# Scaling the FFN input in one VectorE step, and a block's sums of squares at another place, in a hybrid decoder layer

## The chip, the cores and the metric

One core of one Trainium2 chip. The metric is the device time of one execution in microseconds (us); the kernel before ran three times, and one further execution was profiled.

## What is computed

The whole layer works on 2048 tokens of 1024 channels in float32. The part that matters here is the second half and its border with the first:

```python
x = x + jnp.concatenate([hm, hp], axis=-1) @ w_out      # output projection of the mixer
h = rmsnorm(x, g_ffn)                                   # x * rsqrt(mean(x*x) + EPS) * g
up = causal_dwconv(h @ w_up, w_ffn_conv) + b_ffn_conv   # 1024 -> 5632, conv over 3 tokens
gate, val = up[..., :D_FF], up[..., D_FF:]
x = x + (jax.nn.silu(gate) * val) @ w_down              # 2816 -> 1024
return rmsnorm(x, final_norm)
```

## The kernel before, in words

Channels lie on the 128 partitions, tokens along a tile. A tile is 128x512: one of KT = 8 groups of channels (`k`) for one of NB = 4 blocks of 512 tokens (`b`). A float32 product is made of three float32r matmuls (`products`, L112 to L114), since each operand is split in a rounded part (a cast on ScalarE, `split_h`, L94) and a rest (a subtraction on VectorE, `split_l`, L100). So every operand of TensorE costs one ScalarE and one VectorE step first; the split tiles are called `whl` (weights of the first half), `w` (weights of the FFN) and `s` (activations of the FFN).

**Order of the work.** Everything is issued by hand in one program order. TensorE's loops call `tick()` every few matmuls; each tick runs one step of every side stream, a Python generator (`sides`). `yield from wait(n)` puts a stream n ticks back, `until(flag)` holds it, `need(flag)` ticks until a flag is set. What the ticks issue stands in the engines' in-order queues in that order, and semaphores do the rest.

**Mixer and its end.** For each block `in_phase` projects the input; `out_proj(b)` then multiplies with `w_out` in two halves of four channel groups, each in its own PSUM bank `big` (there are four). `evacuate` (L948) adds the residual, loaded as `xr` (three buffers), and a DMA of ScalarE writes the sum to the DRAM scratch `x2d`. `squares` then squares the tile into the same `big` bank (L919) and adds it to `ss` (L923, L925): the bank is free for the next product only after that addition. With all eight tiles added, `scale2` turns `ss` into the scale 1/sqrt(mean) (`spread_rsqrt`: a matmul with ones, then Ln, Exp and Square on ScalarE) and writes it to `r2d`. For the last block `ss` goes to scratch `s2d`, and `last_scale` makes the scale 100 ticks later, in the middle of the first up part.

**FFN.** Tokens are taken in two halves of 1024, in the order `up_half(0)`, `down(0)`, `down(1)`, `up_half(1)`, `down(2)`, `down(3)`. An up part is a Strassen-like scheme with seven products (A11, S1, S2, A12, S3, A22, S4) for each of 22 groups of output channels. Product A11 goes to a bank that `after` copies (ScalarE, L1359) before S2 adds to the same bank, so S2 waits for that copy. The operands of the seven products are 28 tiles. `b_first` makes them for the first half, during `out_proj(3)`, in whose first half `at` starts it: it loads the scale `rr` and 16 tiles of `x2d`, multiplies each with its channel weight and with `rr` (`b_scale`: a ScalarE step, L1138, and a GpSimd step, L1139), subtracts (`sub`, L1142, four of them on GpSimd) and splits. `b_prep(1)` does the same for the second half, during `down(1)`. `a_prep` loads and splits the operands of the down parts, `w_stream` those of the weights, up to nine ahead.

**End.** `squares2` squares and adds each finished output tile, each step after the one before it; `final` scales a block and writes it out. For the last block `down_last` computes the last channel group in two pieces of 256 tokens, and `final_part` scales all eight groups of a piece: five in one VectorE step each, three (1, 3, 5) with a ScalarE copy made earlier and a GpSimd step.

The change touches `out_proj`, `b_scale`, `sub`, `b_first`, `b_prep`, `last_scale`, `down`, `down_last`, `final_part` and `squares2`.

## Time and profile before

| | |
|---|---|
| Median of three runs | 2073.81 us (2069.91 to 2076.69) |
| The profiled execution | 2070.96 us |
| Its span, first to last instruction | 2069.2 us |
| PE matmul busy | 1986.1 us, 96%, x8948 |
| DVE (VectorE) busy | 1457.3 us, 70%, x2330 |
| ACT (ScalarE) busy | 1047.1 us, 51%, x1844 |
| POOL (GpSimd) busy | 236.5 us, 11%, x266 |
| Mean granted clock | 0.984 |

One execution was recorded. Times in rows are us from the span's start; engines are PE, DVE, ACT, POOL, and SP, whose queue issues most DMAs. "L948" is line 948 of the kernel. Matmuls overlap: a 128x512 one is listed with 0.39 us, and in full flow the next begins 0.23 us later. Busy shares are means over stages with different limits. The releaser behind an idle time is the instruction whose end allowed the next to start.

### The profile page before, as it was taken

The numbers are of one execution on the slowest core, as the hardware profiler recorded it, in microseconds if no ns is written. First come the engines' busy times: TensorE is split into PE (matmuls) and PEld (weight loads), VectorE is DVE, ScalarE is ACT, GpSimd is POOL, SyncE is SP. The second block draws the span as 40 slices with busy tenths as digits, with TensorE's granted clock in tenths as the row PEclk, the third lists the DMA queues.
The fourth block names the chain that finished last, engine by engine and source line by source line (L and its number), as shares of the span: only waits on it lengthen the run. The fifth ranks groups of instructions, "written<-read, shape, count | busy, mean of one in ns | idle before, by whom it ended". The sixth has DMA issues, their size and how long they took to land.

```text
span 2069.2 us, 24627 instructions
## 1 busy us (share of the span) xinstructions
PE 1986.1 (96%) x8948; PEld 1628.5 (79%) x8948; DVE 1457.3 (70%) x2330; ACT 1047.1 (51%) x1844; POOL 236.5 (11%) x266
## 2 busy tenths in 40 slices
PE   8999999998998699999999999989999999999997
PEld 6777877776886588788888888877888888888886
DVE  6587777777686977777878656577787787765433
ACT  5656655655644554544455444354455445544331
POOL 1004002012021500000000001120111111000001
PEclk9999999999999799999999999999999999999999
DMA  5433443452346313122224745432322222474441
GB/s 189 151 107 116 153 153 121 133 170 67 113 133 227 113 57 107 66 92 92 69 84 147 253 160 183 143 103 104 104 67 92 92 71 83 133 271 159 150 120 54
DMA packets 116954, 258.64 MB, mean 125 GB/s; under 512 B 9568, under 2 KB 27488, under 8 KB 116832
## 3 DMA queue, kind: packets, MB, share of 16 engines
q1 hardware_dynamic: 111504, 247.37, 36.2%
q10 hardware_dynamic: 5328, 9.70, 1.2%
q8 instruction: 70, 1.15, 0.2%
q14 instruction: 52, 0.43, 0.1%
HBM read 215.81 MB, written 41.22 MB: 124 GB/s over the span
## 4 chain that ended last, share of the span: by engine, by line
PE 77%; DVE 11%; ACT 5%; DMA 4%; issue 2%; SPq 1%; DVEq 0%; POOL 0%; ACTq 0%; POOLq 0%
PE big L112 21%; PE big L113 21%; PE big L114 21%; PE num L114 4%; PE num L113 4%; PE num L112 4%; DVE whl L100 1%; DVE s L100 1%; ACT hjunk L819 1%; DMA x<-x2d 1%; DVE tmp L519 1%; PE mm L503 1%; DVE w L100 1%; DVE hT L102 1%; ACT whl L94 1%
## 5 line engine op out<-in xcount | busy, mean ns | idle before, releaser
L112 PE MATMUL big<-s,w 128*128 128x512 f32 (+1 forms) x1562 | 609.3, 390 | 29.7 <-ACT r L1359 17.6
L114 PE MATMUL big<-s,w 128*128 128x512 f32 (+1 forms) x1562 | 606.7, 388 | 0.0
L113 PE MATMUL big<-s,w 128*128 128x512 f32 (+1 forms) x1562 | 606.5, 388 | 0.0
L94 ACT CAST w<-raw 128x512 fp32r<-128x512 f32 (+1 forms) x442 | 272.7, 619 | 502.8 <-PE big L114 378.1
L100 DVE TENSOR_TENSOR w<-raw,w 128x512 fp32r<-128x512 f32 (+1 forms) x442 | 306.2, 695 | 219.6 <-ACT w L94 214.5
L112 PEld LDWEIGHTS big<-s,w 128*128 128x128 f32 x1562 | 295.6, 189 | 94.3 <-ACT r L1359 19.6
L114 PEld LDWEIGHTS big<-s,w 128*128 128x128 f32 x1562 | 295.4, 189 | 60.5
L113 PEld LDWEIGHTS big<-s,w 128*128 128x128 f32 x1562 | 295.7, 189 | 59.4 <-issue 0.7
L1331 DVE SCALAR_TENSOR_TENSOR q<-q,vec 128x1024 f32<-128x1024 f32 x176 | 225.4, 1281 | 22.2 <-ACT q L1328 20.7
L112 PE MATMUL num<-s,w 128*128 128x512 f32 x396 | 154.7, 391 | 0.0
L114 PE MATMUL num<-s,w 128*128 128x512 f32 x396 | 154.2, 389 | 0.0
L113 PE MATMUL num<-s,w 128*128 128x512 f32 x396 | 154.1, 389 | 0.0
L112 PE MATMUL big<-hT,whl 128*128 128x512 f32 x320 | 130.3, 407 | 15.0 <-DVE ss L925 6.9
L100 DVE TENSOR_TENSOR whl<-wraw,whl 128x1024 fp32r<-128x1024 f32 x92 | 117.3, 1275 | 31.3 <-ACT whl L94 30.2
L100 DVE TENSOR_TENSOR s<-x,s 128x512 fp32r<-128x512 f32 x120 | 83.4, 704 | 70.6 <-ACT s L94 70.1
L113 PE MATMUL big<-hT,whl 128*128 128x512 f32 x320 | 127.9, 400 | 0.6 <-DVE hT L102 0.6
L114 PE MATMUL big<-hT,whl 128*128 128x512 f32 x320 | 127.7, 399 | 0.5 <-DVE whl L100 0.5
L94 ACT CAST s<-x 128x512 fp32r<-128x512 f32 x120 | 72.9, 619 | 106.1 <-PE big L114 48.0
L1328 ACT ACTIVATE q<-q,vec 128x1024 f32<-128x1024 f32 x88 | 109.4, 1243 | 0.0
L1352 POOL COPY q<-halo 128x2 f32<-128x2 f32 x88 | 64.4, 749 | 362.5 <-DVE q L1331 295.8
L112 PE MATMUL big<-whl,hT 128*128 128x512 f32 x256 | 105.0, 410 | 0.0
L113 PE MATMUL big<-whl,hT 128*128 128x512 f32 x256 | 101.9, 398 | 1.4 <-DVE whl L100 1.4
(268 smaller groups left out, 3002.4 us busy)
## 6 DMA issues: line engine op xcount, KB each, us to landing
raw<-in_w_up SPq DMA_DIRECT2D x44, 1024.0 KB, 5.7
raw<-in_w_down SPq DMA_DIRECT2D x35, 1024.0 KB, 5.1
wraw<-in_w_in SPq DMA_DIRECT2D x60, 512.0 KB, 3.3
act<-q SPq DMA_DIRECT2D x44, 512.0 KB, 6.5
x<-act SPq DMA_DIRECT2D x88, 256.0 KB, 3.9
wraw<-in_w_out SPq DMA_DIRECT2D x32, 512.0 KB, 3.3
xr<-in_xT SPq DMA_DIRECT2D x32, 256.0 KB, 4.1
x2d<-xr ACTq DMA_DIRECT2D x32, 256.0 KB, 2.9
```

The source lines that it names most:

```text
L94: act.copy(out=h, in_=src)
L100: dve.tensor_tensor(out=l, in0=src, in1=f(h), op=ALU.subtract)
L102: dve.scalar_tensor_tensor(out=l, in0=src, scalar=scale, in1=f(h), op0=ALU.mult, op1=ALU.subtract)
L112: pe.matmul(o, lhsT=lh, rhs=rh, start=first and i == 0, stop=False, skip_group_check=on)
L113: pe.matmul(o, lhsT=lh, rhs=rl, start=False, stop=False, skip_group_check=on)
L114: pe.matmul(o, lhsT=ll, rhs=rh, start=False, stop=last and i == n - 1, skip_group_check=on)
L503: pe.matmul(gp, lhsT=wg[:, k], rhs=hT[k][:, i], start=k == 0 and i == 0, stop=k == KT - 1 and i == 1)
L519: dve.scalar_tensor_tensor(out=y, in0=pre[:, n:n + BT], scalar=tap[n], in1=y, op0=ALU.mult, op1=ALU.add)
L819: act.activation(junk, nums[h // 2][:, h % 2, 0:DV], AF.Square, scale=rd[:, h:h + 1], accum_out=ssq[:, h:h + 1])
L1328: act.activation(y[gv], pre[gv][:, 2:2 + HT], AF.Identity, scale=tap[2], bias=vec[:, V_FB + ch:V_FB + ch + 1])
L1331: dve.scalar_tensor_tensor(out=y[gv], in0=pre[gv][:, n:n + HT], scalar=tap[n], in1=y[gv], op0=ALU.mult, op1=ALU.add)
L1352: pool.tensor_copy(t[:, 0:2], halo[:, gv * NJ + j])
```

## The change

In order of the program:

- The last block's squares leave `out_proj(3)`; `s2d`, its store, its load and `last_scale` go. Instead `late_scale(3)`, started with `down(0)`, loads the eight tiles of `x2d` again, one every five ticks into two buffers, squares (ScalarE) and adds (VectorE) them, makes the scale and sets the flag `r2`, for which `b_prep(1)` now waits.
- `b_scale` is one VectorE step (`scalar_tensor_tensor`: tile times channel weight times scale) in place of a ScalarE and a GpSimd one, 32 times in all. The four subtractions on GpSimd go to VectorE.
- `b_first` issues its loads six ticks after its start instead of at once, and scales, subtracts and splits in one stream.
- `squares2` no longer waits for the step before it, but four ticks, and adds a tick later.
- The last scaling takes eight VectorE steps; the three ScalarE copies and GpSimd steps go.

```diff
                 if k == KT - 1:
-                    flags.add(("ss", b))
-                    if b < NB - 1:
-                        sides.add(scale2(b, state["ss"], "prs"))
-                    else:
-                        act.dma_start(s2d, state["ss"])
+                    sides.add(scale2(b, state["ss"], "prs"))
...
                     act.dma_start(x2d[k // 2][b][:, k % 2], xr[k])
-                    sides.add(squares(k, o))
+                    if b < NB - 1:
+                        sides.add(squares(k, o))
...
         def b_scale(x, k, r):
-            act.activation(x, x, AF.Copy, scale=vec[:, V_FFN + k:V_FFN + k + 1])
-            pool.tensor_tensor(out=x, in0=x, in1=r, op=ALU.mult)
...
+            dve.scalar_tensor_tensor(out=x, in0=x, scalar=vec[:, V_FFN + k:V_FFN + k + 1], in1=r, op0=ALU.mult, op1=ALU.mult)
...
         def b_first():
-            rr = [ff1.tile([P, 2, 512], F32, tag=f"w{NW1 - 1}", name="rr")]
+            yield from wait(6)
+            rr = ff1.tile([P, 2, 512], F32, tag=f"w{NW1 - 1}", name="rr")
...
             load(0)
             load(1)
-            yield from wait(2)
-            sides.add(scaled())
-            yield from wait(5)
+            yield from wait(3)
...
                 if p < 4:
-                    yield from until("x2", p, kk)
+                    if kk == 0 and p < 2:
+                        load(2 + p)
+                    kh, a = XS[p]
+                    b_scale(x[p, kk], kk + 4 * kh, rr[:, a])
...
                 elif p == S2:
-                    sub(x[1, kk], x[2, kk], x[1, kk], pool)
+                    sub(x[1, kk], x[2, kk], x[1, kk])
...
         def b_prep(hh):
+            yield from until("r2", NB - 1)
...
         out_proj(NB - 1, at)
-        need("ss", NB - 1)
...
-        def last_scale():
-            r = ff2.tile([P, BT], F32, tag="ss", name="r")
-            sp.dma_start(r, s2d)
-            yield from wait(100)
-            yield from spread_rsqrt(r, f(ones_r), [r])
-            act.dma_start(r2d[NB - 1], r)
-        sides.add(last_scale())
+        def late_scale(b):
+            def load(k):
+                t = ff2.tile([P, 512], F32, tag=f"r{1 + k % 2}", name="t")
+                sp.dma_start(t, x2d[k // 2][b][:, k % 2])
+                return t
+            s, t = ff2.tile([P, 512], F32, tag="r0", name="s"), load(0)
+            for k in range(KT):
+                after = load(k + 1) if k + 1 < KT else None
+                yield from wait(3)
+                act.activation(t if k else s, t, AF.Square)
+                yield
+                if k:
+                    dve.tensor_tensor(out=s, in0=t, in1=s, op=ALU.add)
+                t = after
+                yield
+            yield from spread_rsqrt(s, f(ones_r), [s], (6, 2, 1, 1))
+            act.dma_start(r2d[b], s)
+            flags.add(("r2", b))
...
             sides.add(acc_load())
+            if b == 0:
+                sides.add(late_scale(NB - 1))
...
-            for k in (1, 3, 5):
-                x = acc[k // 2][:, k % 2]
-                need("sq", b, k)
-                act.activation(x, x, AF.Copy, scale=vec[:, V_FIN + k:V_FIN + k + 1])
...
-                if k in (1, 3, 5):
-                    pool.tensor_tensor(out=x, in0=x, in1=r, op=ALU.mult)
-                else:
-                    dve.scalar_tensor_tensor(out=x, in0=x, scalar=vec[:, V_FIN + k:V_FIN + k + 1], in1=r, op0=ALU.mult, op1=ALU.mult)
+                dve.scalar_tensor_tensor(out=x, in0=x, scalar=vec[:, V_FIN + k:V_FIN + k + 1], in1=r, op0=ALU.mult, op1=ALU.mult)
...
-                yield from until("sq", b, k - 1)
-                ss = state["ss"]
+                yield from until("sq", b, 0)
+                yield from wait(4)
                 slot = yield from take("mm")
                 o = bank([P, BT])
                 act.activation(o, x, AF.Square)
                 yield
-                dve.tensor_tensor(out=ss, in0=o, in1=ss, op=ALU.add)
+                yield
+                dve.tensor_tensor(out=state["ss"], in0=o, in1=state["ss"], op=ALU.add)
```

How the order of instructions moves, at three places. The lines after the change are numbered a few lower.

**SP's queue at the start of `b_first`**, in the first half of `out_proj(3)`: before.

```order
L1034 DMA raw<-in_w_up 128x2x1024
L937 DMA xr<-in_xT 128x512 x2
L1150 DMA rr<-r2d_89 128x512
L1150 DMA rr<-r2d_90 128x512
L1160 DMA xh<-x2d_0_73 128x512 x2
L1160 DMA xh<-x2d_0_77 128x512 x2
L1160 DMA xh<-x2d_1_74 128x512 x2
L1160 DMA xh<-x2d_1_78 128x512 x2
L226 DMA wraw<-in_w_out 128x1024
L937 DMA xr<-in_xT 128x512 x2
```

Now:

```order
L1030 DMA raw<-in_w_up 128x2x1024
L932 DMA xr<-in_xT 128x512 x2
L225 DMA wraw<-in_w_out 128x1024
L932 DMA xr<-in_xT 128x512 x2
L225 DMA wraw<-in_w_out 128x1024
L932 DMA xr<-in_xT 128x512
L1146 DMA rr<-r2d_89 128x512
L1146 DMA rr<-r2d_90 128x512
L1156 DMA xh<-x2d_0_73 128x512 x2
```

The next weights (`wraw`) and three more residual tiles (`xr`) stand ahead of the ten loads of scale and tiles, no longer behind them.

**DVE, first operands of the FFN** (`s`), in the second half of `out_proj(3)`: before.

```order
L100 TENSOR_TENSOR s<-xh,s 128x512
L100 TENSOR_TENSOR whl<-wraw,whl 128x1024
L100 TENSOR_TENSOR s<-xh,s 128x512
L925 TENSOR_TENSOR ss<-big,ss 128x512
L100 TENSOR_TENSOR s<-xh,s 128x512
L1142 TENSOR_TENSOR xh<-xh 128x512
L100 TENSOR_TENSOR s<-xh,s 128x512
L100 TENSOR_TENSOR whl<-wraw,whl 128x1024
L1142 TENSOR_TENSOR xh<-xh 128x512
L100 TENSOR_TENSOR s<-xh,s 128x512
L1142 TENSOR_TENSOR xh<-xh 128x512
L100 TENSOR_TENSOR s<-xh,s 128x512
```

Now (L1134 is the new scaling, L1137 the subtraction):

```order
L1134 SCALAR_TENSOR_TENSOR xh<-xh,vec,rr 128x512 x2
L100 TENSOR_TENSOR s<-xh,s 128x512
L1134 SCALAR_TENSOR_TENSOR xh<-xh,vec,rr 128x512
L100 TENSOR_TENSOR s<-xh,s 128x512
L100 TENSOR_TENSOR whl<-wraw,whl 128x1024
L1134 SCALAR_TENSOR_TENSOR xh<-xh,vec,rr 128x512
L100 TENSOR_TENSOR s<-xh,s 128x512
L1134 SCALAR_TENSOR_TENSOR xh<-xh,vec,rr 128x512
L1137 TENSOR_TENSOR xh<-xh 128x512
L100 TENSOR_TENSOR s<-xh,s 128x512
L1134 SCALAR_TENSOR_TENSOR xh<-xh,vec,rr 128x512
L1137 TENSOR_TENSOR xh<-xh 128x512
```

The additions to `ss` are gone, and a scaling step stands ahead of each subtraction.

**ACT at the border of `down(1)` and `up_half(1)`**: before (L1553 are the squares of `squares2`, L1359 the copy of A11, which stands behind the fourth of them).

```order
L94 CAST w<-sum 128x512
L1553 ACTIVATE mm<-q 128x512
L94 CAST s<-x 128x512
L94 CAST w<-raw 128x512
L1553 ACTIVATE mm<-q 128x512 x2
L94 CAST w<-raw 128x512
L1553 ACTIVATE mm<-q 128x512
L1359 COPY r<-big 128x512
```

Now:

```order
L94 CAST w<-sum 128x512
L94 CAST s<-x 128x512
L94 CAST w<-raw 128x512 x2
L1359 COPY r<-big 128x512
L1550 ACTIVATE mm<-q 128x512 x2
L94 CAST w<-raw 128x512
L1550 ACTIVATE mm<-q 128x512 x2
```

The copy now stands ahead of the four squares, behind one more cast of weights.

## Rows read from the trace of the kernel before

**Rows 1.** Busy time by stretch: us, then per engine busy us (instructions), granted clock, DMA share, GB/s

```profile
650.00:700.00 50.00, 35.79 (x145) 28.23 (x144) 39.50 (x40) 24.61 (x40) 27.38 (x18) 0.89 0.63 221
...
700.00:750.00 50.00, 40.29 (x155) 32.56 (x156) 42.05 (x62) 26.93 (x46) 5.48 (x10) 0.83 0.21 74
...
800.00:900.00 100.00, 95.88 (x409) 78.32 (x409) 75.47 (x96) 52.27 (x75) 3.40 (x16) 0.97 0.23 76
...
900.00:1000.00 100.00, 100.00 (x442) 82.64 (x441) 76.71 (x98) 49.90 (x73) 5.55 (x24) 1.00 0.29 94
...
1300.00:1400.00 100.00, 92.93 (x403) 76.54 (x402) 63.83 (x89) 45.28 (x77) 20.82 (x16) 0.97 0.33 113
...
705.00:722.00 17.00, 12.29 (x35) 9.46 (x36) 16.97 (x29) 10.69 (x20) 0.00 (x0) 0.70 0.37 127
...
1120.00:1140.00 20.00, 20.00 (x90) 16.57 (x89) 18.19 (x26) 15.65 (x26) 0.87 (x4) 1.00 0.69 236
```

**Rows 2.** Timeline, PE, 662 to 1396: start, us, operation, [idle before <- releaser]

```profile
670.90 0.79 PE L112 MATMUL big<-hT,whl 128*128 128x512 f32 x1 [6.93 <-DVE ss L925]
...
705.34 0.80 PE L112 MATMUL big<-s,w 128*128 128x512 f32 x1 [12.15 <-DVE ss L925]
...
717.49 0.80 PE L112 MATMUL big<-s,w 128*128 128x512 f32 x1 [4.37 <-ACT r L1359]
...
864.51 0.79 PE L112 MATMUL big<-s,w 128*128 128x512 f32 x1 [4.12 <-ACT r L1359]
...
1395.34 0.80 PE L112 MATMUL big<-s,w 128*128 128x512 f32 x1 [7.07 <-ACT r L1359]
```

**Rows 3.** Timeline, SP's DMA queue, 648 to 664

```profile
651.36 10.20 SPq L1160 DMA_DIRECT2D xh<-x2d  x8
...
662.10 0.91 SPq L937 DMA_DIRECT2D xr<-in_xT  x2
```

**Rows 4.** Timeline, DVE, 650 to 720

```profile
650.54 1.23 DVE L100 TENSOR_TENSOR whl<-wraw,whl 128x1024 fp32r<-128x1024 f32 x1 [0.19 <-ACT whl L94]
...
658.94 0.68 DVE L948 TENSOR_TENSOR xr<-big,xr 128x512 f32<-128x512 f32 x1
...
672.50 0.80 DVE L100 TENSOR_TENSOR s<-xh,s 128x512 fp32r<-128x512 f32 x1 [0.45 <-ACT s L94]
...
709.41 0.67 DVE L100 TENSOR_TENSOR s<-xh,s 128x512 fp32r<-128x512 f32 x1
```

**Rows 5.** Groups by form, DVE, 661.4 to 704.1: xcount | busy us, mean ns

```profile
L100 DVE TENSOR_TENSOR s<-xh,s 128x512 fp32r<-128x512 f32 x12 | 15.8, 1316 | 0.5 <-ACT s L94 0.5
...
L1142 DVE TENSOR_TENSOR xh<-x,xh 128x512 f32<-128x512 f32 x4 | 6.4, 1604 | 0.0
```

**Rows 6.** DMA issues, 640 to 720: xcount, KB each, median us to landing

```profile
x2d<-xr ACTq DMA_DIRECT2D x8, 256.0 KB, 2.7
...
xh<-x2d SPq DMA_DIRECT2D x12, 256.0 KB, 4.5
```

**Rows 7.** Timeline, DVE, 1412 to 1419: the operation that the new scaling uses

```profile
1415.84 1.41 DVE L1572 SCALAR_TENSOR_TENSOR q<-q,vec,rn 128x512 f32<-128x512 f32 x2
```

**Rows 8.** Timeline, ACT, 714 to 718

```profile
716.85 0.58 ACT L1359 COPY r<-big 128x512 f32<-128x512 f32 x1
```

**Rows 9.** Timeline, ACT, 857 to 866

```profile
858.38 1.28 ACT L167 ACT_TABLE_LOAD   x1
...
860.35 1.28 ACT L168 ACT_TABLE_LOAD   x1
```

**Rows 10.** Timeline, ACT, 1371 to 1396

```profile
1372.07 0.72 ACT L1138 ACTIVATE x<-x,vec 128x512 f32<-128x512 f32 x1 [0.43 <-DMA x<-x2d]
...
1392.37 0.60 ACT L1553 ACTIVATE mm<-q 128x512 f32<-128x512 f32 x1 [2.77 <-DVE ss L1555]
```

**Rows 11.** Timeline, DVE, 1385 to 1388

```profile
1386.73 1.28 DVE L1451 TENSOR_TENSOR q<-big,q 128x512 f32<-128x512 f32 x2
```

**Rows 12.** Timeline, DVE, the last scaling, 2060 to 2066

```profile
2062.14 3.57 DVE L1534 SCALAR_TENSOR_TENSOR q<-q,vec,rn 128x256 f32<-128x256 f32 x5
```

More of the change, by code (lines that the diff above doesn't have):

```diff
@@ L197, in trunk @@
         r2d = [dram.tile([P, BT], F32, name=f"r2d{b}") for b in range(NB)]
-        s2d = dram.tile([P, BT], F32, name="s2d")
         per = tc.alloc_tile_pool(name="per", bufs=1, side="left", reuse_waits="tile")
@@ L1137, in b_scale, with sub @@
         def b_scale(x, k, r):
-            act.activation(x, x, AF.Copy, scale=vec[:, V_FFN + k:V_FFN + k + 1])
-            pool.tensor_tensor(out=x, in0=x, in1=r, op=ALU.mult)
-        def sub(o, a, b, eng=dve):
-            eng.tensor_tensor(out=o, in0=a, in1=b, op=ALU.subtract)
+            dve.scalar_tensor_tensor(out=x, in0=x, scalar=vec[:, V_FFN + k:V_FFN + k + 1], in1=r, op0=ALU.mult, op1=ALU.mult)
+        def sub(o, a, b):
+            dve.tensor_tensor(out=o, in0=a, in1=b, op=ALU.subtract)
         XS = ((0, 0), (0, 1), (1, 1), (1, 0))
         def b_first():
-            rr = [ff1.tile([P, 2, 512], F32, tag=f"w{NW1 - 1}", name="rr")]
+            yield from wait(6)
+            rr = ff1.tile([P, 2, 512], F32, tag=f"w{NW1 - 1}", name="rr")
             for a in range(2):
-                sp.dma_start(rr[0][:, a], r2d[a])
+                sp.dma_start(rr[:, a], r2d[a])
             held = [ff1.tile([P, 2, 512], F32, tag=f"s{HOLD + i}", name="xh") for i in range(6)]
@@ L1160, in load @@
                     sp.dma_start(x[i, kk], x2d[k // 2][a][:, k % 2])
-            def scaled():
-                for i, (kh, a) in enumerate(XS):
-                    if i + 2 < 4:
-                        load(i + 2)
-                    for kk in range(4):
-                        b_scale(x[i, kk], kk + 4 * kh, rr[0][:, a])
-                        flags.add(("x2", i, kk))
-                        if (i, kk) == (1, 3):
-                            raw_load(1)
-                        if (i, kk) == (3, 3):
-                            rr.clear()
-                            flags.add(("rr",))
-                        yield
             load(0)
             load(1)
-            yield from wait(2)
-            sides.add(scaled())
-            yield from wait(5)
+            yield from wait(3)
             last = None
@@ L1190, in b_first @@
                 if p < 4:
-                    yield from until("x2", p, kk)
+                    if kk == 0 and p < 2:
+                        load(2 + p)
+                    kh, a = XS[p]
+                    b_scale(x[p, kk], kk + 4 * kh, rr[:, a])
+                    if n == 4:
+                        raw_load(1)
+                    if n == 15:
+                        del rr
+                        flags.add(("rr",))
                 if p == S1:
@@ L1502, in down_last @@
                             tick()
-                need("sq", b, k - 1)
+                for i in range(k):
+                    need("sq", b, i)
                 x = acc[k // 2][:, k % 2]
@@ L1554, in squares2 @@
                 yield
-                dve.tensor_tensor(out=ss, in0=o, in1=ss, op=ALU.add)
+                yield
+                dve.tensor_tensor(out=state["ss"], in0=o, in1=state["ss"], op=ALU.add)
                 give(slot)
@@ L1559, in squares2 @@
                 assert b < NB - 1
+                for i in range(k):
+                    yield from until("sq", b, i)
                 sides.add(final(b, acc))
```

## The prediction, made before the changed kernel had run

> **What bounds the kernel now.** I read the busy time by stretch first. TensorE is the bound: in a full stretch 442 matmuls end in 100 us, one in 0.226 us, at a granted clock of 1.00 [rows 1]. So each stretch with fewer tells what is lost there, idle time and slow clock together: (442 - 145 - 155) x 0.226 = 32 us from 650 to 750, (442 - 409) x 0.226 = 7.5 us from 800 to 900, (442 - 403) x 0.226 = 8.8 us from 1300 to 1400 [rows 1]. The change works on these three places and on the end. The timeline of TensorE then names what ended each idle time: additions to `ss` at 670.90 and 705.34, the copy of A11 at 717.49, 864.51 and 1395.34 [rows 2]. From 717.49 on no idle time follows until 860, so the time at which that copy lets S2 start is what the first place is worth.
>
> **Place 1, the border to the FFN.** Behind the copy stands a chain on VectorE: the first sixteen FFN operands, whose first split starts at 672.50 and the sixteenth at 709.41 [rows 4], 36.9 us for 33 operations by the order. VectorE works there almost without a pause. While GpSimd works (27.38 us of 650 to 700), twelve splits take 1316 ns each and four subtractions 1604 [rows 1, 5]; with GpSimd silent, 29 operations pass in 17.0 us, 0.60 each [rows 1], the split at 709.41 in 0.67 [rows 4]. So GpSimd's steps stretch VectorE's.
>
> What is removed from this chain: GpSimd's steps, and the additions to `ss`. What is added: 14 scalings and 4 subtractions. One 128x512 `scalar_tensor_tensor` from SBUF is listed with 0.70 (two in 1.41), and the next begins 0.67 after it [rows 7]. By the new order 46 operations stand between the first and the sixteenth split: 14 scalings x 0.67, 15 splits, 12 subtractions and 4 evacuations x 0.60, and one weight split of twice the length, 1.2 (as at 650.54 [rows 4]): 9.4 + 18.6 + 1.2 = 29.2 us, against 36.9.
>
> When does it start? The loads are issued later, but now three residual tiles go ahead of them. Before, eight tile loads held SP's queue 10.20 us from 651.36, and the next residual tiles left at 662.10 [rows 3]; that made the evacuation late that held TensorE until 670.90 [rows 2]. Now the last residual load ahead of the FFN's waits for the write of the second sum: evacuated at 658.94, about 659.7 issued, landed 2.7 later [rows 4, 6], 662.4. Two loads of the scale and the first tile take some 0.4 of the queue each: 663.6. A tile lands 4.5 after issue [rows 6]: 668. With one scaling (0.67) and a cast by ScalarE (0.6) the first split starts at 669, 3.5 earlier than now. The sixteenth then starts at 669 + 29.2 = 698.2.
>
> Between this and the copy ScalarE now has three casts; before there were ten entries, among them the store of `ss`, behind the last addition: 709.41 to 716.85 is 7.4 us [rows 4, 8]. Now it is some 2. S2 starts at 700.5 in place of 717.49: **17 us**. TensorE will have finished the output projection at about 684 (now 705.34 - 12.15 = 693.2, less the idle 6.93 and the slow clock behind it [rows 2]), then does A11 and S1 and waits some 10 us: it still pays for a slow clock afterwards, as now. Bounds: loads that land 10 us later, as a full queue [rows 3] could make them, leave 7; if VectorE held nothing up, S2 would start when TensorE has done A11 and S1, 24 x 0.226 after 684, at 689.5, a gain of 28. I take the walk's value, since each of its lengths has a row.
>
> **A rule against this.** Rows 1 and 5 show VectorE full and ScalarE with half its time free. The Trainium skill, "Perfetto Trace Analysis", section "Optimizing Scalar/DVE Operations", says that when DVE is saturated, moving work to Scalar or even GPSIMD may make sense; the change does the reverse. By that rule the chain is only longer by the 18 operations added: it is the rival of VectorE below. The same section adds that GPSIMD and DVE share an SBUF read port, so moving work between these two might not help; the 1316 ns against 0.67 us side with that half of it.
>
> **Place 2, the scale of the last block.** In the middle of `up_half(0)` ScalarE loads two tables, 1.28 us each, for Ln and Exp [rows 9], with the copy of A11 behind them, and TensorE idles 4.12 us until 864.51 [rows 2]; with the slow clock 7.5 are lost. The matmul with ones moves to `down(0)` and costs its 0.5 there. **7 us**, if nothing is paid in `down(0)`. What moves there: 8 loads, 8 squares (0.60 each, as at 1392.37 [rows 10]), 7 additions (0.60) and the scale. They wait on their engines in front of weight casts; `down` has no copy that TensorE needs at once, and weights are split up to nine items of 12 matmuls ahead (2.7 us each). VectorE is busy 18.19 of 20 us at 1120 to 1140, where it begins, with TensorE full [rows 1]. Bounds: the same 7 lost again (gain 0), or all 7.5.
>
> **Place 3, `down(1)` to `up_half(1)`.** The copy stands behind four squares, the third of which waits 2.77 us for an addition [rows 10]; it ends the idle 7.07 at 1395.34 [rows 2]. Now it stands ahead of them. But `b_prep`'s scalings join VectorE. From 1372.1, where the second of the last four tiles lands [rows 10], 19 operations stand before the evacuation: 3 x 0.67 + 16 x 0.60 = 11.6, so 1383.7 instead of 1386.73 [rows 11]; 8 more (4.8) give the source of a weight cast, and cast and copy take 1.2: 1389.7. TensorE is ready at 1395.34 - 7.07 = 1388.3: 1.4 idle instead of 7.07, and less slow clock. **6.5 us** of the 8.8; bounds 0 and 8.8.
>
> **Place 4, the end.** Five VectorE steps take 3.57 us beside GpSimd's three [rows 12]; eight at 0.35 to 0.42, an estimate from half the elements of a 0.67 step and its fixed part, take 2.8 to 3.4. Twice: **0.5 us**, bounds 0 and 1.5.
>
> **At nothing:** `squares2` in the other down parts (TensorE loses nothing there, rival 3 is what it costs if the lead is gone), the wait of `b_prep(1)` for `r2` (set after some 50 of the 88 ticks of `down(0)`, while `b_prep` begins only when `a_prep(1)` has ended, whose operand slots come free till near the end of `down(0)`), the removed store and load of `s2d`.
>
> **Sum.** 17 + 7 + 6.5 + 0.5 = 31 us. Against the profiled execution: 2070.96 - 31 = 2040. That execution is 2.9 below the median of the runs; I give 2042.
>
> **Rivals.**
> 1. *Late tiles.* VectorE's queue is in order, so a scaling that waits for its tile now holds the evacuations and a weight split behind it too; before, ScalarE and GpSimd waited. For: DMA was 0.63 busy over 650 to 700 [rows 1] and 4 MB must pass. Against: three residual tiles and two weights have gone ahead. Each us late costs one; 10 late gives 2052.
> 2. *VectorE bound (slower).* If the long operations are not GpSimd's doing, the chain becomes longer: 41 of the 46 at the 1.6 us of the subtractions [rows 5] are 66, with the 5 others 69 instead of 29; S2 starts at 740.5, 23 us later than now, and 14 gained elsewhere leave it 9 slower, 2083 beside the median. It decides where those 41 take more than 1.37 us each. This is where the rule above leads. Against: 0.60 each as soon as GpSimd is silent [rows 1].
> 3. *A stall that moves.* `late_scale` starves `down(0)`, or VectorE, with 20 operations added in `b_prep`, keeps place 3 as it is: 7 less, 2049.
> 4. *Nothing there.* TensorE's wait at place 1 passes from `ss` to the operands with the copy as late as now; only places 2 to 4 remain: 2060.
>
> **How the numbers follow.** The sum as it stands 0.60, late tiles 0.14, a stall that moves 0.13, nothing at place 1 0.06, VectorE bound 0.05, no difference at all 0.02. The sum's own bounds, without the extremes together, reach from 2032 to 2050. To hold eight in ten the range goes from 2030 to 2058: late tiles and moved stalls are in it, rivals 2 and 4 are not. What can be told from no change is about 0.3%, 6 us: faster 0.92, same 0.03, slower 0.05.
>
> **What would show it.** Right: no DVE operation of 128x512 over 0.8 us at 650 to 750; S2's wait for the copy ends near 700; no idle time of TensorE at 860; the wait at the next border 1 to 3 us; `down(0)` full. Wrong: TensorE idle during the output projection behind a weight split (late tiles), or a wait in `down(0)`.

## The result

| | before | after |
|---|---|---|
| Median of four runs | 2073.36 us (2069.91 to 2076.69) | 2042.29 us (2040.55 to 2042.69) |
| The profiled execution, its span | 2070.96 us, 2069.2 | 2040.55 us, 2038.8 |
| PE matmul busy | 1986.1 us | 1975.6 us, 97%, x8948 |
| DVE busy | 1457.3 us | 1455.3 us, x2371 |
| ACT busy | 1047.1 us | 1023.2 us, x1808 |
| POOL busy | 236.5 us | 175.1 us, x224 |
| Mean granted clock | 0.984 | 0.992 |

The ratio of after to before is 0.9849, 95% interval 0.9837 to 0.986: 31 us faster, 2042 forecast. VectorE executes 41 instructions more than before and is busy no longer.

### The profile page after: what moved, and what is told of

The parts are those of the page before. It is cut to its first block, busy times and chain, and to the rows that moved or that the text cites. A ratio compares the mean times of both kernels' runs of the same rounds, so it can differ in the third digit from the quotient of the medians.

```text
span 2038.8 us, 24551 instructions
## 1 busy us (share of the span) xinstructions
PE 1975.6 (97%) x8948; PEld 1621.2 (80%) x8948; DVE 1455.3 (71%) x2371; ACT 1023.2 (50%) x1808; POOL 175.1 (9%) x224
## 4 chain that ended last, share of the span: by engine, by line
PE 80%; DVE 10%; ACT 5%; DMA 2%; issue 2%; SPq 1%; POOL 0%; DVEq 0%; ACTq 0%; POOLq 0%
PE big L112 21%; PE big L113 21%; PE big L114 21%; PE num L114 5%; PE num L113 5%; PE num L112 5%; DVE whl L100 1%; DVE tmp L518 1%; ACT hjunk L818 1%; ACT whl L94 1%; PE mm L502 1%; DVE hT L102 1%; DMA tmp<-in_x 1%; DVE s L100 1%; DVE xh L1137 0%
## 5 line engine op out<-in xcount | busy, mean ns | idle before, releaser
L100 DVE TENSOR_TENSOR w<-raw,w 128x512 fp32r<-128x512 f32 (+1 forms) x442 | 301.6, 684 | 198.1 <-ACT w L94 192.9
```

The lines of the kernel that those rows point to most:

```text
L100: dve.tensor_tensor(out=l, in0=src, in1=f(h), op=ALU.subtract)
```

## The profile after, against the rows of before

Busy time by stretch of the changed kernel (columns as in [rows 1]), and below it the one stretch of the kernel before that was not among the rows:

```profile
650.00:700.00 50.00, 40.33 (x174) 32.05 (x172) 40.82 (x61) 16.09 (x24) 0.47 (x3) 0.97 0.67 242
700.00:750.00 50.00, 45.22 (x185) 36.81 (x186) 42.77 (x65) 29.35 (x49) 1.85 (x8) 0.89 0.23 74
800.00:900.00 100.00, 100.00 (x442) 82.75 (x441) 77.88 (x101) 48.86 (x72) 4.96 (x21) 1.00 0.28 87
1300.00:1400.00 100.00, 100.00 (x441) 82.44 (x440) 78.20 (x123) 44.68 (x78) 0.00 (x0) 1.00 0.32 111
1400.00:1450.00 50.00, 49.17 (x218) 40.38 (x217) 42.66 (x54) 26.68 (x39) 8.02 (x6) 1.00 0.36 118
1160.00:1180.00 20.00, 20.00 (x90) 16.57 (x89) 13.31 (x22) 11.57 (x22) 0.00 (x0) 1.00 0.81 264
```

```profile
1400.00:1450.00 50.00, 47.98 (x210) 39.03 (x209) 38.73 (x53) 24.18 (x37) 0.86 (x3) 1.00 0.27 100
```

Matmuls per stretch are the measure, 0.226 us each at full flow. From 650 to 750 there are 174 + 185 = 359 in place of 300 [rows 1]: 59, or 13.3 us, are won at place 1. From 800 to 900 it is 442 against 409: 33, 7.5 us, place 2. From 1300 to 1450 it is 441 + 218 = 659 against 403 + 210 = 613: 46, 10.4 us, place 3, of which 8 matmuls lie behind 1400, where nothing had been forecast. The last matmul of the output starts 12.3 us ahead of the end (2026.51, span 2038.8) and did so 12.7 us ahead of it (2056.45, span 2069.2): 0.5 us, place 4. The sum is 31.7, less 5 matmuls (1.1 us) by which this execution came later to 650, in a part that the change leaves alone (2909 matmuls from 0 to 650 in place of 2914): 30.6. The spans differ by 30.4.

The timeline of TensorE, with its idle times of more than 0.5 us between 640 and 2026 (columns as in [rows 2]):

```profile
691.08 0.47 PE L112 MATMUL big<-s,w 128*128 128x512 f32 x1 [2.84 <-DVE xr L943]
...
704.51 0.80 PE L112 MATMUL big<-s,w 128*128 128x512 f32 x1 [10.46 <-ACT r L1359]
...
1419.45 0.50 PE L112 MATMUL big<-s,w 128*128 128x512 f32 x1 [0.83 <-ACT r L1359]
```

S2 starts at 704.51 instead of 717.49. The idle times at 864.51 and 1395.34 [rows 2] have no counterpart. The one at 1419.45 is what is left of one of 2.02 at 1443.85 in the kernel before.

VectorE's chain at place 1 and the queue ahead of it, in the timelines of DVE, SP and ACT:

```profile
670.79 1.41 DVE L1134 SCALAR_TENSOR_TENSOR xh<-xh,vec,rr 128x512 f32<-128x512 f32 x2 [2.47 <-DMA xh<-x2d]
672.23 0.69 DVE L100 TENSOR_TENSOR s<-xh,s 128x512 fp32r<-128x512 f32 x1
...
701.68 1.46 DVE L100 TENSOR_TENSOR s<-xh,s 128x512 fp32r<-128x512 f32 x2
```

```profile
663.91 7.51 SPq L1156 DMA_DIRECT2D xh<-x2d  x8
```

```profile
703.88 0.57 ACT L1359 COPY r<-big 128x512 f32<-128x512 f32 x1
```

S2's copy starts at 703.88. The chain runs from the split at 672.23 to the second of the two at 701.68, without an operation over 0.75 us but the weight split. Twelve splits took 1316 ns each before [rows 5]. Where [rows 3] show eight loads holding the queue 10.20 us, they now hold it 7.51, behind the residual tile. But the first scaling waits 2.47 us for its tile, which lands 6.9 us after 663.91 and not 4.5.

Places 2, 3 and 4, in the timelines of ACT (1190 to 1200 and 1365 to 1375) and DVE (the end):

```profile
1192.27 1.28 ACT L167 ACT_TABLE_LOAD   x1
...
1194.24 1.28 ACT L168 ACT_TABLE_LOAD   x1
...
1367.38 0.58 ACT L1359 COPY r<-big 128x512 f32<-128x512 f32 x1
1367.86 1.12 ACT L1550 ACTIVATE mm<-q 128x512 f32<-128x512 f32 x2
```

```profile
2031.94 3.25 DVE L1530 SCALAR_TENSOR_TENSOR q<-q,vec,rn 128x256 f32<-128x256 f32 x8
```

The two table loads [rows 9] now stand in `down(0)`, where nothing waits behind them: TensorE is busy 20.00 of 20 us in each such stretch from 1100 to 1240. The copy of A11 stands ahead of the squares. Eight scalings take 3.25 us where five took 3.57 [rows 12].

## Experiments

Each was timed in four executions beside the kernel before on the same chip; on the three chips used, the kernel before took 2072.2 to 2072.6 us. The changed kernel was not timed there again. A difference of less than some 3 us between two medians tells nothing. "After" is the median 2042.29, and 359 its matmuls from 650 to 750.

### 1. GpSimd work that nobody needs

```diff
 def b_first():
+    idle = mix.tile([P, BT], F32, tag="ss", name="idle")
     yield from wait(6)
+    pool.memset(idle, 1.0)
...
     yield from wait(3)
+    for i in range(16):
+        pool.tensor_tensor(out=idle, in0=rr[:, i % 2], in1=idle, op=ALU.mult)
```

> The changed kernel with sixteen GpSimd multiplications added in the first operands' stage, on a tile that nothing else uses (the bank of sums of squares of the mixer, free by then). They start when the scale has landed, at about 669 us, and nothing waits for their values. Theory (GpSimd's steps stretch VectorE's): while they run, some 16 x 1.5 = 24 us, a 128x512 split or subtraction takes 1.2 us or more in place of 0.68 and some 20 operations pass in place of 40, so the copy that starts S2 comes 10 to 14 us later than 703.88 and the time is about 2053. Rival (the long operations before were something else, such as DMA traffic or the additions from PSUM): the steps stay at 0.68 and the time within 2 us of 2042.

Measured: 2057.56 us (2056.67 to 2058.0), 15.3 slower. Groups by form of DVE from 669 to 697, then its timeline around the end of GpSimd's work, then that work (POOL), as a row of its timeline and as a summary of its line (least, median and greatest ns):

```profile
L1134 DVE SCALAR_TENSOR_TENSOR xh<-xh,vec,rr 128x512 f32<-128x512 f32 x6 | 10.6, 1774 | 2.7 <-DMA xh<-x2d 2.7
L100 DVE TENSOR_TENSOR s<-xh,s 128x512 fp32r<-128x512 f32 x5 | 8.8, 1758 | 0.0
```

```profile
695.51 1.75 DVE L100 TENSOR_TENSOR s<-xh,s 128x512 fp32r<-128x512 f32 x1
697.18 0.74 DVE L1134 SCALAR_TENSOR_TENSOR xh<-xh,vec,rr 128x512 f32<-128x512 f32 x1
...
698.57 0.69 DVE L100 TENSOR_TENSOR s<-xh,s 128x512 fp32r<-128x512 f32 x1
```

```profile
670.24 26.47 POOL L1163 TENSOR_TENSOR idle<-rr,idle 128x512 f32<-128x512 f32 x16 [12.10 <-DMA rr<-r2d]
```

```profile
L1163 POOL TENSOR_TENSOR idle<-rr,idle x16: 1288/1605/2131, 670.2 to 695.1; 128x512 f32<-128x512 f32 x16
```

The stretch is GpSimd's doing: same operations, same data, 1.76 us a split, and 0.69 from the moment GpSimd stops. From 650 to 750, 291 matmuls end, 68 fewer than after: 15.4 us. VectorE's steps follow each other every 1.68 us (695.51 to 697.18) and not every 0.60, GpSimd's every 1.65 (26.47 / 16): the two take turns. So one GpSimd multiplication costs VectorE 1.68 - 0.60 = 1.08 us, where VectorE has a step with two SBUF operands ready at every moment, as here.

### 2. The same with copies, which read one operand

```diff
-    for i in range(16):
-        pool.tensor_tensor(out=idle, in0=rr[:, i % 2], in1=idle, op=ALU.mult)
+    for i in range(24):
+        pool.tensor_copy(idle, rr[:, i % 2])
```

> As the run with the sixteen idle GpSimd multiplications, but with 24 copies of the landed scale into the same unused tile: one operand read in place of two. It tells whether any GpSimd work stretches VectorE's steps or only work that reads two tiles. Theory (any GpSimd step that reads SBUF stretches them): 128x512 splits of 1.2 us or more as long as the copies run; if the copies take 1 us each, 24 us of them, the time is near 2055. Rival (only two-operand steps do): 0.7 us a split, 2040 to 2045.

Measured: 2049.9 us (2048.41 to 2051.56). Neither expectation holds; it lies between. The instructions of the copy's line, and DVE's timeline:

```profile
L1163 POOL COPY idle<-rr x24: 617/953/1487, 671.1 to 693.6; 128x512 f32<-128x512 f32 x24
```

```profile
677.22 1.09 DVE L1134 SCALAR_TENSOR_TENSOR xh<-xh,vec,rr 128x512 f32<-128x512 f32 x1
678.23 1.09 DVE L100 TENSOR_TENSOR s<-xh,s 128x512 fp32r<-128x512 f32 x1
```

A step of VectorE now comes every 1.02 us: a copy costs it 0.42. Alone, GpSimd's copy takes 0.62 (the least in the row) and its multiplication 1.29 (the least of experiment 1); with VectorE's 0.60 that is 1.22 and 1.89, and both pitches, 1.02 and 1.68, are 0.2 below. So both fit one reading: what counts is how long the GpSimd step is, and a copy with one operand stretches VectorE too.

### 3. The first half's scaling on ScalarE and GpSimd again

```diff
 def b_first():
     yield from wait(6)
+            def scaled():
...
+                        b_scale_pool(x[i, kk], kk + 4 * kh, rr[0][:, a])
...
-                    b_scale(x[p, kk], kk + 4 * kh, rr[:, a])
+                    yield from until("x2", p, kk)
...
-                    sub(x[1, kk], x[2, kk], x[1, kk])
+                    sub_pool(x[1, kk], x[2, kk], x[1, kk])
```

`b_scale_pool` is the scaling of the kernel before (a ScalarE and a GpSimd step), `sub_pool` a subtraction on GpSimd, `scaled` the stream that the change had removed; all else is as after.

> The changed kernel with the scaling of the first sixteen tiles as before (ScalarE copy with the channel weight, GpSimd multiplication, in a stream of their own) and the four subtractions of S2 on GpSimd again; the loads stay late, the last block's squares stay in the first down part, and the second half's scaling stays on VectorE. Theory (place 1 is won by taking GpSimd away): VectorE has 18 operations fewer, but its splits take 1.3 us while GpSimd works; S2 starts at 711 to 717 instead of 704.5, the time is 2049 to 2055. Rival (place 1 is won by the removed additions of squares and the order of the loads): S2 starts at 698 to 706 and the time is 2036 to 2044.

Measured: 2049.48 us (2048.22 to 2051.92), 7.2 slower. Stretches; TensorE's start of S2; and one evacuation of VectorE (L943, which reads one operand from PSUM) beside the GpSimd step under way:

```profile
650.00:700.00 50.00, 43.66 (x186) 33.92 (x184) 35.28 (x37) 21.57 (x34) 22.07 (x14) 1.00 0.71 247
700.00:750.00 50.00, 35.48 (x140) 27.39 (x141) 46.18 (x61) 28.32 (x49) 12.44 (x14) 0.83 0.13 48
```

```profile
712.00 0.80 PE L112 MATMUL big<-s,w 128*128 128x512 f32 x1 [13.23 <-ACT r L1374]
```

```profile
701.26 0.68 DVE L943 TENSOR_TENSOR xr<-big,xr 128x512 f32<-128x512 f32 x1
```

```profile
700.75 1.71 POOL L1146 TENSOR_TENSOR xh<-x,xh 128x512 f32<-128x512 f32 x1
```

186 + 140 = 326 matmuls, 33 fewer than after: 7.5 us of place 1 come from taking these steps off ScalarE and GpSimd. Here it is VectorE that is full: 26 operations take 32.99 us of it from 672 to 711, while after the change 49 take 31.82 from 670.8 to 703. By the prices of experiment 1: 20 GpSimd steps would take 20 x 1.08 = 21.6 us from VectorE, 16 scalings and 4 subtractions of its own take 16 x 0.67 + 4 x 0.60 = 13.1, the difference is 8.5. That is an upper estimate, since some GpSimd steps ran beside an evacuation or in a pause of VectorE. The evacuation takes 0.68 with GpSimd at work beside it, so a step with only one operand in SBUF is not stretched.

### 4. Only the scaling and the subtractions changed, all else as before

```diff
 def b_scale(x, k, r):
-    act.activation(x, x, AF.Copy, scale=vec[:, V_FFN + k:V_FFN + k + 1])
-    pool.tensor_tensor(out=x, in0=x, in1=r, op=ALU.mult)
+    dve.scalar_tensor_tensor(out=x, in0=x, scalar=vec[:, V_FFN + k:V_FFN + k + 1], in1=r, op0=ALU.mult, op1=ALU.mult)
...
-    sub(x[1, kk], x[2, kk], x[1, kk], pool)
+    sub(x[1, kk], x[2, kk], x[1, kk])
```

> The kernel before, with nothing changed but the scaling step of both halves (one VectorE step) and the four subtractions of S2 (VectorE). Theory: the chain from the first to the sixteenth split keeps the additions of squares and loses GpSimd's stretch, some 30 us in place of 36.9, so S2 starts near 710; the late residual tile (6.93 idle near 670) and the two other stalls stay; 2060 to 2066. Rival 1 (VectorE bound): 2073 or more. Rival 2 (the scaling alone is the whole gain of place 1): 13 to 15 less than before, 2058 to 2060.

Measured: 2061.56 us (2058.06 to 2064.16), 11 faster than the 2072.57 of before beside it; the median is where the theory had it, but not for its reasons alone. TensorE's timeline:

```profile
713.77 0.80 PE L112 MATMUL big<-s,w 128*128 128x512 f32 x1 [3.96 <-ACT r L1358]
...
1384.26 0.50 PE L112 MATMUL big<-s,w 128*128 128x512 f32 x1 [1.89 <-ACT r L1358]
```

S2 starts at 713.77, not near 710, and 149 + 176 = 325 matmuls end from 650 to 750, 25 (5.7 us) more than before. The late residual tile is still there (7.06 idle before 672.61). But the border of `down(1)`, where "the two other stalls stay" was expected, shrank from 7.07 idle to 1.89 without any change to `squares2`: 431 + 212 = 643 matmuls from 1300 to 1450 against 613, 30 or 6.8 us.

### 5. The loads as early as before

```diff
 def b_first():
-    yield from wait(6)
```

> The changed kernel with the loads of scale and tiles, and the scalings behind them, issued six ticks earlier, where the loads stood before. Theory (the order of the queue matters): the tile loads hold the queue some 10 us ahead of the residual tiles, so an evacuation is late and TensorE idles 3 to 7 us near 670, and scalings that wait for tiles hold weight splits; what the chain gains by its earlier start is lost again: 2042 to 2050. Rival (an earlier start of the chain is what counts, since the chain is what ends last): S2 starts 4 to 8 us earlier, 2035 to 2038.

Measured: 2043.25 us (2042.33 to 2045.57), not to be told from after. TensorE's timeline:

```profile
685.01 0.79 PE L112 MATMUL big<-hT,whl 128*128 128x512 f32 x1 [3.79 <-ACT whl L94]
...
707.25 0.50 PE L112 MATMUL big<-s,w 128*128 128x512 f32 x1 [2.40 <-ACT r L1358]
```

S2 now waits 2.40 us and not 10.46, but five idle times of 1.4 to 3.8 us, 10.2 together, stand in the output projection: the loss has moved. 159 + 199 = 358 matmuls, as after. The later issue of the loads is worth nothing by itself.

### 6. The last block's sums and scale as before

```diff
-                    if b < NB - 1:
-                        sides.add(squares(k, o))
+                    sides.add(squares(k, o))
...
-            if b == 0:
-                sides.add(late_scale(NB - 1))
```

`s2d`, its store and load and `last_scale` are back as in the kernel before.

> The changed kernel with the last block's squares in the output projection again, the sums stored and loaded, and the scale made 100 ticks into the first up part. Theory: two losses come back at two places. In the middle of the first up part TensorE idles about 4 us behind the copy that waits for the two table loads, 7.5 us with the slow clock; at the border to the FFN eight additions (0.6 each) lengthen VectorE's chain by up to 5 us and hold the banks. Together 2050 to 2056. Rival (the banks held by the additions were the greater part of place 1): 10 us or more at the border, 2060. Rival 2 (the late scale costs as much in the first down part as it saves): 2042 to 2046.

Measured: 2054.92 us (2052.9 to 2056.91), 12.6 slower. Stretches, and TensorE's timeline in the first up part:

```profile
650.00:700.00 50.00, 39.05 (x160) 30.67 (x159) 42.68 (x64) 19.02 (x30) 1.01 (x3) 0.90 0.67 242
700.00:750.00 50.00, 42.11 (x174) 33.97 (x174) 43.56 (x67) 28.97 (x48) 0.92 (x4) 0.90 0.17 58
800.00:900.00 100.00, 95.88 (x412) 78.46 (x411) 74.08 (x96) 52.17 (x74) 4.63 (x20) 0.97 0.27 85
```

```profile
857.45 0.80 PE L112 MATMUL big<-s,w 128*128 128x512 f32 x1 [4.12 <-ACT r L1353]
```

The theory holds at both places: 160 + 174 = 334 matmuls, 25 fewer (5.6 us) at the border, and 412 from 800 to 900, 30 fewer than 442 (6.8 us), with the idle 4.12 of [rows 2] to a hundredth. The move to `down(0)` costs nothing there.

### 7. The squares of the output in a chain again

```diff
-                yield from until("sq", b, 0)
-                yield from wait(4)
+                yield from until("sq", b, k - 1)
```

The addition again follows one tick after its square.

> The changed kernel with the sums of squares of the outputs as before, each waiting for the one before it. Theory (the place of the copy in ScalarE's queue is what counts at the border of the second down part and the second up part): the copy stands behind four squares again, TensorE idles 4 to 7 us there, 2047 to 2051. Rival (the border was won because the operands of the second half come earlier without ScalarE's and GpSimd's scaling): no idle time, 2041 to 2044.

Measured: 2046.96 us (2044.07 to 2053.4), 4.7 slower. TensorE's timeline at the border, and one up-part group later:

```profile
1371.99 0.50 PE L112 MATMUL big<-s,w 128*128 128x512 f32 x1 [1.26 <-ACT r L1359]
...
1418.74 0.50 PE L112 MATMUL big<-s,w 128*128 128x512 f32 x1 [2.02 <-ACT r L1359]
```

The copy is behind four squares again, yet only 1.26 us are idle at the border. The other idle time is the 2.02 of the kernel before; with the new order it is 0.83. Together 434 + 212 = 646 matmuls from 1300 to 1450 against 659: 13, 2.9 us. The rest of the 4.7 lies in the spread of the runs and at place 1 (176 + 177 = 353 matmuls in this execution, with nothing changed there). So the copy's place is the smaller part of place 3.

### 8. The second half's scaling on ScalarE and GpSimd again

```diff
 def b_prep(hh):
-                    b_scale(x[i], k, rs[a])
+                    act.activation(x[i], x[i], AF.Copy, scale=vec[:, V_FFN + k:V_FFN + k + 1])
+                    pool.tensor_tensor(out=x[i], in0=x[i], in1=rs[a], op=ALU.mult)
```

> The changed kernel with the second half's scaling (sixteen tiles during the second down part) on ScalarE and GpSimd as before; the first half's stays on VectorE. The mirror of the run before it. Theory (the copy's place counts): within 2 us of 2042, the border without idle time or with up to 2 us. Rival (GpSimd's and ScalarE's part in the scaling made the operands late): 4 to 9 us idle at the border, 2047 to 2052.

Measured: 2049.79 us (2047.88 to 2050.82), 7.5 slower: the rival. TensorE's timeline and ScalarE's:

```profile
1374.37 0.56 PE L112 MATMUL big<-s,w 128*128 128x512 f32 x1 [4.59 <-ACT r L1366]
```

```profile
1373.21 0.62 ACT L94 CAST w<-raw 128x512 fp32r<-128x512 f32 x1 [4.38 <-DVE raw L1061]
1373.74 0.58 ACT L1366 COPY r<-big 128x512 f32<-128x512 f32 x1
```

The copy is ahead of the squares and 4.59 us are idle all the same: ScalarE waits 4.38 us for a VectorE step of the weights (L1061), the cast behind which the copy stands, because VectorE is late. 412 + 218 = 630 matmuls from 1300 to 1450, 29 fewer than after, 6.6 us. With the 2.9 of experiment 7 this makes 9.5 of the 10.4 us of place 3.

Why is VectorE late? By the prices of experiment 1, sixteen GpSimd steps cost it 16 x 1.08 and its own scalings 16 x 0.67, a difference of 6.6 too. But this agreement is chance. The stretch from 1300 to 1366 in this run, then in the changed kernel (columns as in [rows 1]; VectorE's is the third busy time):

```profile
1300.00:1366.00 66.00, 66.00 (x293) 54.65 (x292) 45.72 (x64) 33.66 (x59) 20.23 (x16) 1.00 0.35 120
```

```profile
1300.00:1366.00 66.00, 66.00 (x293) 54.66 (x292) 54.23 (x85) 28.39 (x50) 0.00 (x0) 1.00 0.35 120
```

With the scaling on GpSimd VectorE has less to do (45.72 of 66 us in place of 54.23) and is late all the same: it has pauses, and a GpSimd step in a pause costs it nothing. Twelve GpSimd scalings lie in this stretch (the other four of the 16 are short copies); they stretch VectorE's steps by some 5 us together (an estimate: five steps of 1.6 to 1.8 us in place of 0.7, and a few of 0.8 to 0.9), which is less than the 12 x 0.67 = 8.0 of scalings of its own.

What is longer is the round. `b_prep` takes four tiles at a time and issues the next four loads behind their splits. The four scalings take 7.3 us here, from the first ScalarE copy at 1352.56 to the end of the fourth GpSimd step at 1359.8, and 2.75 us on VectorE. The loads of the last four tiles (SP), and the first matmul of A11 at this border (PE), in the kernel before, in this run and in the changed kernel:

```profile
1365.54 2.79 SPq L1226 DMA_DIRECT2D x<-x2d  x4
1382.67 0.39 PE L112 MATMUL big<-s,w 128*128 128x512 f32 x1
```

```profile
1346.82 2.97 SPq L1222 DMA_DIRECT2D x<-x2d  x4
1364.18 0.39 PE L112 MATMUL big<-s,w 128*128 128x512 f32 x1
```

```profile
1343.08 2.88 SPq L1215 DMA_DIRECT2D x<-x2d  x4
1363.17 0.39 PE L112 MATMUL big<-s,w 128*128 128x512 f32 x1
```

The loads start 17.1 us ahead of A11 before, 17.4 here and 20.1 after. The copy of A11 starts 12.0, 9.6 and 4.2 us behind A11's first matmul (at 1394.70, 1373.74 and 1367.38), while TensorE is ready for S2 after 24 x 0.226 = 5.4. So that these scalings are worth 6.6 us is shown, and that they make the rounds shorter. Not shown is how much of a round is the longer way of a tile through two engines and how much VectorE's stretched steps: ScalarE's copies were not tried apart from GpSimd's steps.

### 9. Can what is left at place 1 be had?

From 650 to 750 the changed kernel still loses (442 - 359) x 0.226 = 19 us. Four attempts, the first being early loads through GpSimd's idle queue:

```diff
 def b_first():
-    yield from wait(6)
...
-    sp.dma_start(rr[:, a], r2d[a])
+    pool.dma_start(rr[:, a], r2d[a])
...
-    sp.dma_start(x[i, kk], x2d[k // 2][a][:, k % 2])
+    (pool if i < 2 else sp).dma_start(x[i, kk], x2d[k // 2][a][:, k % 2])
...
-    yield from wait(3)
+    yield from wait(5)
```

> The changed kernel with the loads of the scale and the first eight tiles issued through GpSimd's queue, which is idle there, at the start of the stream (near 650 us), and the first scaling five ticks later, four ticks ahead of where the change has it. Theory (place 1 is now bound by VectorE's chain, and that by the arrival of the tiles, 670.8 us): the tiles land before 662, the chain starts 4 to 6 us earlier, in VectorE's pauses between 651 and 667, S2 starts at 698 to 700 and the time is 2035 to 2038. Rival (the DMA engines are full from 650 to 680, so residual tiles and weights come later by as much): TensorE idles in the output projection behind an evacuation or a weight split, 2041 to 2048.

Measured: 2042.26 us (2039.26 to 2043.84). TensorE's timeline:

```profile
708.61 0.80 PE L112 MATMUL big<-s,w 128*128 128x512 f32 x1 [3.76 <-ACT r L1358]
```

The rival: the DMA engines were 0.99 busy from 650 to 660, the three residual tiles issued there landed 10.4 us after issue in the median, and the first evacuation is at 661.91 (655.86 after). So the first scaling comes only 1.6 us earlier (669.19) and the first split no earlier (672.41). TensorE idles 7.0 us in the output projection, in five waits; S2 waits 3.76 us instead of 10.46 and yet starts 4.1 later than after, and 162 + 192 = 354 matmuls end.

Next, the operands from the thirteenth on held back until the copy of A11 is issued:

```diff
+                if n == 12:
+                    yield from until("after", 0, 0, A11)
                 if p < 4:
```

> The changed kernel, but the first-half stream waits before the thirteenth operand until the copy of A11 is issued, so that on ScalarE the copy stands behind twelve casts and not sixteen; S2's own operands are the ninth to twelfth. Theory (VectorE's chain of all 28 operands bounds the border, wherever S2 starts): S2 starts 6 to 8 us earlier, near 697, but A12, S3 and A22 then wait for their operands, TensorE gets back 1 to 3 us at most: 2039 to 2042. Rival (the wait of S2 is the loss itself): 2034 to 2037. Rival 2 (held operands come later and the wait moves behind S2 with a loss): 2043 to 2046.

Measured: 2042.93 us (2041.28 to 2045.31). TensorE's timeline:

```profile
701.72 0.50 PE L112 MATMUL big<-s,w 128*128 128x512 f32 x1 [2.75 <-ACT r L1361]
...
713.26 0.50 PE L113 MATMUL big<-s,w 128*128 128x512 f32 x1 [2.17 <-DVE s L100]
```

S2's wait falls from 10.46 to 2.75 and nothing is won: the products behind it wait for their own splits, and 182 + 170 = 352 matmuls end, 7 fewer than after. S2's wait was where the loss showed, not what made it. The theory and its second rival both say so; the median lies between their ranges and does not choose between them.

Then the tile loads of the first attempt with the residual tiles ahead of them and the 1 MB of weights behind them:

```diff
-                        at(hf)
                         if hf == 0:
                             load(0)
                             load(1)
+                        at(hf)
...
-                raw_load(0)
                 sides.add(s_stream())
...
-    yield from wait(5)
+    yield from wait(4)
+    raw_load(0)
```

> As the run with the loads on GpSimd's queue, but the two residual tiles go first, the 1 MB of FFN weights four ticks after the tiles instead of ahead of them, and the scalings start four ticks behind the loads. Theory (in that run the transfers of 650 to 660 collided: the first evacuation waited till 661.9 for its residual tile): the evacuation is back at 656 to 657, the chain starts near 662, S2 near 697 to 700, 2035 to 2039. Rival (the place is bound by VectorE's total work, and what comes ahead of the weight splits delays TensorE in the output projection): S2's wait shrinks, as much is idle in the output projection, 2040 to 2045.

Measured: 2047.68 us (2046.96 to 2049.39).

And with the hold added:

> The two runs before this one together. Theory (bound by VectorE's total work): no more than 2 us better than the better of the two. Rival (two separate waits): the gains of both add up, 2030 to 2035.

Measured: 2051.3 us (2047.46 to 2053.91). The first is slower than either side expected: TensorE idles 4.00 us behind an evacuation (before 675.64) and 4.13 behind the cast of a weight (before 686.81), and still 3.89 for S2 (before 711.80). The second gains nothing, as the theory had it, but is slower than both of its parts, which neither side had expected. No version was found that beats the changed kernel.

## Why the prediction was right, and where it was not

The total came out as forecast, 2042.29 for 2042, but by luck: two errors cancel. Place 1 was sized 4 us too high, place 3 4 us too low.

**Place 1: 17 forecast, 13.3 measured; the mechanism right, the start too early.** The chain of 46 operations was to take 29.2 us; from 672.23 to 702.4 it took 30.2 (eight of the scalings have a subtraction of the same tile right behind them, which starts 0.78 after them and not 0.67, as at 676.50 and 677.28). Between its last split and S2 there were to be 2.3 us; there were 2.1. TensorE was to wait some 10 us for S2; it waited 10.46. What failed is the term "a tile lands 4.5 after issue": the loads were issued at 663.91, as forecast to 0.3 us, but the first tile held the scaling up until 670.79, since the 4.5 is the median of the kernel before [rows 6]; the twelve loads of tiles now take 5.7 in the median. That is 3.2 us at the first split, and with the 1.0 of the chain, less 0.2, it makes the 4 us by which S2 came after 700.5. The experiments divide the 13.3: 7.5 for taking the scaling and the four subtractions off ScalarE and GpSimd (3; 5.7 when that is done alone, 4), 5.6 for the removed squares and additions (6), nothing for the order of the loads (5). Rival 1, late tiles, came true to this extent of 3 us. Rival 2, VectorE as the bound with a slower kernel, fell with experiment 1: its point of decision was 1.37 us an operation, and without GpSimd they take 0.60 to 0.67. Rivals 3 and 4 had no part in the result.

**Work moved onto the busy engine.** The Trainium skill, "Perfetto Trace Analysis", "Optimizing Scalar/DVE Operations", states that with a saturated DVE moving some work to Scalar or even GPSIMD may make sense, and that moving it between DVE and GPSIMD might not help, since they share an SBUF read port. The rows of place 1, where VectorE is full, agree with the second half and speak against the first for GpSimd: a scaling done by VectorE costs it 0.67 us, GpSimd's multiplication costs it 1.08 (experiment 1). The Trainium skill, "SBUF — State Buffer", "Who interferes with whom", states that a VectorE instruction with two inputs in SBUF contends with a GpSimd instruction that reads SBUF, and one with at most one such input, outside the 2-port modes, does not: experiments 1 and 3 agree (1.68 beside 0.68 us).

**Place 2: 7 forecast, 7.5 measured,** 6.8 in experiment 6; nothing is paid in `down(0)`. No step of it failed.

**Place 3: 6.5 forecast, 10.4 measured; the start of the last group was wrong.** From 1300 to 1400 it is 38 matmuls, 8.6 us; the other 8 lie behind 1400, where a later copy that TensorE waits for (1443.85 before) became 1.2 us shorter, of which the prediction does not speak. What failed is the start of the walk, "from 1372.1, where the second of the last four tiles lands": a time of the kernel before, kept as if the scalings of the three groups ahead of it had no effect on it. But each group's loads stand behind the splits of the group before, and the last loads came 3.0 us earlier against A11 (20.1 ahead for 17.1, experiment 8). The way from there to S2 was counted 1 us too short. Together, the copy ended 4.8 us behind A11's first matmul where the forecast had 7.0 (1389.7 - 1382.67), ahead of the 5.4 at which TensorE is ready: nothing was idle where 1.4 had been forecast.

So the argument that the copy now stands ahead of the squares is right but is the smaller part: it brings 2.9 (7). The scalings, which the prediction entered only as a load added to VectorE and rival 3 even as what might keep place 3 as it is, bring 6.6 (8; 6.8 in experiment 4).

**Place 4: 0.5 forecast, 0.5 measured.**

Not settled: why the two kernels with the tiles first lose as much as they do. Their TensorE waits are known, but what in the DMA traffic makes them was not tried apart.

## What to carry to other kernels

When two engines slow each other, price a step by what it costs the busy engine, not by which engine runs it: at place 1 a scaling moved to the full VectorE was cheaper for it than the multiplication on GpSimd. Such a price holds only where that engine has no pause. At place 3 VectorE had pauses, and the same move paid because it made each round of loads, scalings and splits shorter; the price gave the right sum there by chance, and only the engine's busy time told the difference. A control that adds useless work to the suspected engine, on data nobody needs, tells such a cost apart from all dependencies in one run. And a long wait names the place of a loss, not its cause: three edits took 7 to 8 us of S2's wait away and the time stayed.

## What had not been expected of the hardware

When both have a step ready, GpSimd and VectorE take turns: with two VectorE operands in SBUF, the pitch of both is the sum of the times that each takes alone, less 0.2 us (1.68 for 0.60 + 1.29; 1.02 for 0.60 + 0.62). A one-operand GpSimd copy, which had been expected either to stretch VectorE as much or not at all, stretches it by its own shorter time.
